# Turning the first two key groups of four attention heads through wider copies, behind the products of the head before

## The chip, the cores and the metric

The kernel runs on one core of a Trainium2 chip. Five engines work on it, each in its own order: PE (TensorE, matrix products and transposes), DVE (VectorE), ACT (ScalarE), POOL (GpSimd) and SP (SyncE, which here issues nearly all DMAs). PE writes to eight PSUM banks; all other tiles lie in SBUF. The metric is the device time of one execution in microseconds (us), and the median of several is compared.

## What is computed

One block of a decoder on x of 1024 tokens by 1024 channels, in float32: attention with a forget gate beside a gated spatial mix, a projection back, and a gated feed-forward network with a short convolution. The part that matters here is the attention, with 8 heads of 64 channels:

```python
def block(args):
    qi, ci, pi = args
    logits = jnp.einsum('bqhd,bkhd->bhqk', qi, k).astype(jnp.float32) * scale
    logits = logits + ci[..., None] - c_k
    causal = pi[:, None] >= key_pos[None, :]
    logits = jnp.where(causal, logits, -jnp.inf)
    p = jax.nn.softmax(logits, axis=-1).astype(v.dtype)
    return jnp.einsum('bhqk,bkhd->bqhd', p, v)
```

The spatial mix and its share of the projection supply independent products that the kernel puts between the attention's own ("filler").

## The kernel before

**Precision.** Products are made of fp32r operands. A float32 value is split into a high part, rounded to fp32r, and the rest (low part); a product is then two or three matmuls.

**One head.** The queries and the keys are cut into 8 blocks of 128. For each query block `j` the logits of its `j + 1` key blocks are two matmuls into PSUM (`logits_mm`, L1021 and L1022), DVE adds the mask and finds the extreme of a row (`logits_min`, L1038), and ACT takes the exponential in place (`logits_exp`, L1062). The rows of the blocks 2i and 2i + 1 lie in one SBUF tile: tags `gg`, `wy`, `t2` and `t3` for i = 0 to 3, in `places`. To multiply them with V, PE has to transpose each 128 x 128 block (`turn_p`): four blocks into one PSUM bank, which ACT casts to the high part (L1094) and DVE subtracts from for the low part (L1095), both into a tile `pt`. Then `values` makes the products with V (L1109), the high part and the low part of a span after each other, into the banks `po`.

**Copies.** A transpose is cheap as fp32r, but an operand of that kind may not be what an engine wrote as float32. So for heads 1 to 7 `copy_p` has SP copy the exponentials by DMA, SBUF to SBUF, into tiles `C2` and `C3` (for i = 2, 3) and new `wy` and `gg` (for i = 1, 0): two DMAs a tile, the odd block of queries first, tile 3 ahead of tile 2. Of `t2` and `t3` only the columns from 256 on are copied (`COLS`). A turn of the first 256 columns, key blocks 0 and 1, for the query blocks 4 to 7 then reads the float32 original with a float32 identity (L1093); all others read the copy as fp32r (L1090).

**The order.** `GROUPS` lists nine groups of turns: key blocks 0 to 7 for the upper half of the queries (the first two are the groups in question), then the lower half. `STEPS` takes two at a time, five steps a head, 40 in all. Step n of the loop at L1226 (head `h`, place `s`) issues the turns of step n + 1, then the products of step n, each followed by logits of head h + 1 (`NEXT`), then exponentials, copies (`due_copies`: tiles 3 and 2 at s = 2, tile 1 at s = 3, tile 0 at s = 4) and, in the places of `FILLS`, one filler of 12 matmuls (L1143 to L1145) with its evacuation (L1147, L1148). At s = 4 stand the turns of head h + 1's first two groups (8 transposes), the four products of the last group (two of 384 columns, two of 128) and a filler. PE keeps the written order (`seq`). On the other engines and on SP a scheduler orders the instructions by its own estimate of when they can run, with some pairs fixed by `after`.

**Also on SP**: `head_loads` (L895 to L908), the filler's residual loads `raw<-xtok` (L1125) and, for each head, the broadcast of the reciprocal row sums from DRAM into `H` (L975), behind ACT's write of them to `rsd` (L974).

**Buffers.** `C2` and `C3` have one buffer each, `pt` three, and the turns, `po` and the row tail share four PSUM banks.

Of the kernel before, what the change touches and what calls it, by code (L numbers as in the profile page):

```python
# [14 lines left out]
P = 128  # L15
# [59 lines left out]
def block_kernel(ctx: ExitStack, tc: tile.TileContext, xT, xtok, wuv, wuh, wv0, wva, wvk, wvl, wqk, cpk, bfv,  # L75
# [225 lines left out]
    for o in (slice(0, 256), slice(256, 512)):  # L301
        h, l, src = xs("B11", 0, 0)[:, o], xs("B11", 1, 0)[:, o], xr("x11", 0)[:, o]
# [657 lines left out]


    TTAG = ("gg", "wy", "t2", "t3")
    COLS = (0, 0, 2, 2)
    CTAG = ("gg", "wy", "C2", "C3")
    exs, turns, due_copies, copied = [], {}, [], []

    def row_tail(h):

        p, hh, rs = h // 2, h % 2, rows[h]
        ptr = bank()  # L970
        rt = idr[0:8, 640 + P * hh:640 + P * (hh + 1)]
        seq(pe.transpose(ptr[0:8, 0:P], rs, ident))
        act.copy(rt, ptr[0:8, 0:P])
        act.dma_start(out=rsd[h], in_=rt)  # L974
        sp.dma_start(out=attF[p][hh * 64:hh * 64 + 64, 1, :],  # L975
                     in_=rsd[h].rearrange("a b -> (a b)").unsqueeze(0).to_broadcast((64, 1024)))
# [71 lines left out]
    def copy_p(h, i, ld=None):  # L1048

        w1, w2 = (2 * i + 1) * P, (2 * i + 2) * P  # L1050
        c = COLS[i] * P
        w1, w2 = w1 - c, w2 - c
        tp = sb(CTAG[i], [P, w1 + w2])
        turns[h, i] = (tp[:, 0:w1], tp[:, w1:w1 + w2])
        for jj in (1, 0):
            copied[:] = [sp.dma_start(out=turns[h, i][jj], in_=places[h, i][jj][:, c:])]
            if ld:
                after(tc, copied[0], ld)
# [21 lines left out]
    def turn_p(g):  # L1080

        ptr = bank()
        pt = sb("pt", [P, 2, 512], F32R)
        for half, k, j0, c, w in spans(g):
            for j in range(j0, 4 * half + 4):
                o = c + (j - j0) * P
                kc = k - COLS[j // 2]
                if kc >= 0 and (g[0], j // 2) in turns:
                    t = turns[g[0], j // 2][j % 2][:, kc * P:(kc + 1) * P]
                    seq(pe.transpose(ptr[:, o:o + P].bitcast(F32R), t.bitcast(F32R), identr))  # L1090
                else:
                    t = places[g[0], j // 2][j % 2][:, k * P:(k + 1) * P]
                    seq(pe.transpose(ptr[:, o:o + P], t, ident))  # L1093
        casts.append(act.copy(pt[:, 0, :], ptr))  # L1094
        los.append(dve.tensor_tensor(out=pt[:, 1, :], in0=ptr, in1=f32(pt[:, 0, :]), op=ALU.subtract))  # L1095
        return pt
# [93 lines left out]
    STEPS = [[(h, g) for g in GROUPS[n:n + 2]] for h in range(8) for n in range(0, 9, 2)]  # L1190
# [34 lines left out]
    turned = [turn_p(g) for g in STEPS[0]]  # L1225
    for n, step in enumerate(STEPS):  # L1226
        h, s = n // 5, n % 5
        if s == 0 and h < 6:
            head_loads(h + 2)
        if h == 7 and s == 0:  # L1230
            for _ in filler:
                pass
            wo_load((0, 1))
            wo_load((2, 3))
        if h in (2, 4, 6) and s == 4:
            for o in (slice(0, 512), slice(512, 1024)):
                pair_half(h // 2 - 1, o)
        now, turned = turned, []
        last, due = due, []
        if n == 0:  # L1240
            fill((0, 0))
        if n == 35:
            psl.release()
            psl = tc.alloc_tile_pool(name="psc", bufs=4, space=bass.MemoryType.PSUM, reuse_waits="tile")
            banks8[0, 0] = lbank()
            wmm(0, 0, banks8[0, 0], (0,))
        for g in STEPS[n + 1] if n + 1 < len(STEPS) else []:
            if n == 36 and turned:
                for e in held + [mrow]:
                    after(tc, logits_exp(*e), casts[-1])  # L1250
            turned.append(turn_p(g))
            if n == 36 and len(turned) == 2:
                after(tc, casts[-1], exs[-1])
        if n == 34:
            mrow = (7, 0, logits_min(7, 0, mrow))
        if n == 33:

            held, last = last, []
        if n == 34:
            last, held = held[:1], held[1:] + last  # L1260
        if n == 35:
            last, held = held[:1], held[1:]
        if s == 1 and h % 2 == 0:
            attF[h // 2] = sb("H", [P, 2, 1024])
        if s == (1 if h < 7 else 2):
            recips[h] = dve.reciprocal(rows[h], rows[h])
        out_copy = None
        if n in EARLY:
            wmm(0, 0, banks8[0, 0], EARLY[n])
        if n == 37:  # L1270
            row_tail(7)
        if n == 39:
            banks8[4, 0] = lbank()
            wmm(4, 0, banks8[4, 0], (0,))
        for c, (g, pt, js) in enumerate(zip(step, now, NEXT[s])):
            out_copy = values(g, pt) or out_copy
            last_copy = out_copy
            if h < 7:
                for j in js:
                    if n == 33 and j == 0:  # L1280
                        mrow = logits_mm(7, 0, place())
                        continue
                    due.append((h + 1, j, logits_min(h + 1, j, logits_mm(h + 1, j, place()))))
            if s == 1 and h < 7 and c == 0:
                row_tail(h)

        for e in last:
            x = logits_exp(*e)
            after(tc, x, casts[-1] if n == 34 else out_copy or casts[-1])
        if s == 2 and h < 7:  # L1290
            due_copies.extend(((h + 1, 3), (h + 1, 2)) if h < 6 else ((7, 3),))
        if n:
            fill((h, s))
        if s > 2 and h < 6:
            due_copies.append((h + 1, 4 - s))
        while due_copies:
            copy_p(*due_copies.pop(0))
        for _ in range(min(len(SPLIT), 1 if n == 9 else 2)):
            ws_, k, wr = SPLIT.pop(0)
            wt = sb("whl", [P, 2, 512], F32R)  # L1300
            ws_[k] = wt
            after(tc, act.copy(wt[:, 0], wr), out_copy or casts[-1])
            pool.tensor_tensor(out=wt[:, 1], in0=wr, in1=f32(wt[:, 0]), op=ALU.subtract)
        if n == 2:
            vh = sb("A", [P, 2, 4, 256])
            sp.dma_start(out=vh, in_=vu.rearrange("h p m c -> p h m c"))
        if n in UPPER:
            tt = UPPER.index(n)
            v = V[tt // 2][:, tt % 2, 4:8]
            src = vh[:, tt // 4, tt % 4, :].rearrange("p (h d) -> p h d", h=4)  # L1310
            after(tc, act.activation(src, src, AF.Copy, scale=rstd1[:, tt:tt + 1]), exs[-1])
            pool.tensor_copy(v[:, :, 0, :], src)
            pool.tensor_tensor(out=v[:, :, 1, :], in0=src, in1=f32(v[:, :, 0, :]), op=ALU.subtract)
# [631 lines left out]
```

## Time and profile before

| | us |
|---|---|
| three runs, median (lowest to highest) | 1041.49 (1040.13 to 1042.59) |
| the profiled execution | 1041.76 |
| its span, first to last instruction | 1039.7 |
| PE busy | 1031.3 (99%) |
| DVE busy | 889.1 (86%) |
| ACT busy | 564.5 (54%) |
| POOL busy | 242.2 (23%) |

The eight heads lie between about 223 and 358 us of the span. In a timeline a row has its start, its length, the engine, the line of the kernel, the operation, the tile written and the tiles read, the shape and the count. Matmuls overlap, so the step between the starts of two rows tells more than their lengths. "SPq" rows are instructions that SP issues. In the rows on DMA the GB/s line has the stretch in 40 equal slices.

### The profile page before, as it was taken

The numbers are of one execution on the slowest core, as the hardware profiler recorded it, in microseconds if no ns is written. First come the engines' busy times: TensorE is split into PE (matmuls) and PEld (weight loads), VectorE is DVE, ScalarE is ACT, GpSimd is POOL, SyncE is SP. The second block draws the span as 40 slices with busy tenths as digits, with TensorE's granted clock in tenths as the row PEclk, the third lists the DMA queues.
The fourth block names the chain that finished last, engine by engine and source line by source line (L and its number), as shares of the span: only waits on it lengthen the run. The fifth ranks groups of instructions, "written<-read, shape, count | busy, mean of one in ns | idle before, by whom it ended". The sixth has DMA issues, their size and how long they took to land.

```text
span 1039.7 us, 14434 instructions
## 1 busy us (share of the span) xinstructions
PE 1031.3 (99%) x4998; PEld 865.5 (83%) x4998; DVE 889.1 (86%) x1294; ACT 564.5 (54%) x1004; POOL 242.2 (23%) x195
## 2 busy tenths in 40 slices
PE   9999999999999999999999999999999999999997
PEld 6988888988888888888888888888888888888886
DVE  6899887888888888998999998998997857997774
ACT  6777533467876757654444443444544554444654
POOL 0000242412633540343334323332331000000000
PEclk9999999999999999999999999999999999999999
DMA  9622558887878652231454332432322998333432
GB/s 336 222 97 82 162 147 245 235 265 225 267 250 255 231 171 93 82 122 62 142 172 144 131 110 72 132 102 89 114 82 94 330 329 293 108 92 101 150 116 100
DMA packets 73708, 170.25 MB, mean 164 GB/s; under 512 B 8718, under 2 KB 12934, under 8 KB 73636
## 3 DMA queue, kind: packets, MB, share of 16 engines
q1 hardware_dynamic: 73364, 169.30, 49.9%
q8 instruction: 39, 0.64, 0.2%
q14 instruction: 33, 0.27, 0.1%
q10 hardware_dynamic: 272, 0.04, 0.0%
HBM read 112.53 MB, written 45.05 MB: 152 GB/s over the span
## 4 chain that ended last, share of the span: by engine, by line
PE 98%; DVE 1%; DMA 1%; issue 0%; SPq 0%; ACT 0%; DVEq 0%
PE pb L1491 23%; PE pk L1491 17%; PE pb L1755 11%; PE pk L1755 9%; PE ps L286 5%; PE pb L286 5%; PE pk L1185 4%; PE pb L1109 3%; PE qc L525 2%; PE qd L525 2%; PE qa L525 2%; PE ps L876 2%; PE pl L1021 1%; PE pl L1022 1%; PE pf L1143 1%; PE pf L1144 1%
## 5 line engine op out<-in xcount | busy, mean ns | idle before, releaser
L1491 PE MATMUL pb<-xT,whb 128*128 128x512 f32 x804 | 189.4, 389 | 0.0
L1491 PEld LDWEIGHTS pb<-xT,whb 128*128 128x128 f32 x804 | 150.9, 188 | 31.4
L1491 PE MATMUL pk<-xB,x 128*128 128x512 f32 x528 | 127.2, 390 | 0.0
L1755 PE MATMUL pb<-whb,x 128*128 128x512 f32 (+1 forms) x528 | 119.2, 387 | 0.0
L1491 PEld LDWEIGHTS pk<-xB,x 128*128 128x128 f32 x528 | 98.8, 188 | 20.8 <-DVE x L175 0.4
L1755 PEld LDWEIGHTS pb<-whb,x 128*128 128x128 f32 x528 | 98.3, 188 | 20.3 <-DVE x L175 0.2
L169 ACT CAST x<-sg 128x512 fp32r<-128x512 f32 x77 | 47.8, 622 | 96.7 <-PE pk L1755 46.1
L169 ACT CAST whb<-sg 128x512 fp32r<-128x512 f32 x82 | 50.5, 617 | 84.8 <-PE pb L1491 83.8
L1755 PE MATMUL pk<-whb,x 128*128 128x512 f32 (+1 forms) x408 | 91.8, 386 | 0.0
L1755 PEld LDWEIGHTS pk<-whb,x 128*128 128x128 f32 x408 | 75.9, 188 | 15.5
L175 DVE TENSOR_TENSOR x<-sg,x 128x512 fp32r<-128x512 f32 x77 | 52.7, 687 | 38.7 <-ACT x L169 38.6
L1541 DVE SCALAR_TENSOR_TENSOR ca<-h,cp,ca 128x1023 f32<-128x1023 f32 (+1 forms) x44 | 68.2, 1550 | 3.7 <-ACT ca L1540 3.6
L1541 DVE SCALAR_TENSOR_TENSOR cg<-h,cp,cg 128x1023 f32<-128x1023 f32 (+1 forms) x44 | 65.2, 1482 | 5.8 <-ACT cg L1540 5.5
L1491 PE MATMUL pb<-xB,whb 128*128 128x512 f32 x264 | 63.9, 389 | 0.0
L175 DVE TENSOR_TENSOR whb<-sg,whb 128x512 fp32r<-128x512 f32 x82 | 57.4, 701 | 4.4 <-ACT whb L169 4.3
L1491 PE MATMUL pk<-xT,whb 128*128 128x512 f32 x252 | 61.0, 389 | 0.0
L1388 POOL TENSOR_TENSOR sg<-raw 128x512 f32<-128x512 f32 x20 | 29.8, 1489 | 131.5 <-DVE whb L175 72.7
L1094 ACT CAST pt<-pb 128x512 fp32r<-128x512 f32 x72 | 40.4, 583 | 33.0 <-PE pb L1090 20.7
L1491 PEld LDWEIGHTS pb<-xB,whb 128*128 128x128 f32 x264 | 49.5, 188 | 10.7 <-issue 0.4
L1095 DVE TENSOR_TENSOR pt<-pb,pt 128x512 fp32r<-128x512 f32 x72 | 47.5, 687 | 11.1 <-ACT pt L1094 10.3
L1491 PEld LDWEIGHTS pk<-xT,whb 128*128 128x128 f32 x252 | 47.2, 188 | 10.0 <-DVE whb L175 0.3
L1109 PE MATMUL pb<-pt,V 128*128 128x512 f32 (+3 forms) x192 | 49.0, 360 | 0.0
(425 smaller groups left out, 2165.7 us busy)
## 6 DMA issues: line engine op xcount, KB each, us to landing
raw<-wup SPq DMA_DIRECT2D x44, 512.0 KB
sg<-hx SPq DMA_DIRECT2D x77, 256.0 KB
hx<-hs SPq DMA_DIRECT2D x44, 256.0 KB
hx<-ca SPq DMA_DIRECT2D x35, 256.0 KB
xT<-wdn SPq DMA_DIRECT2D x28, 256.0 KB
x<-kd SPq DMA_DIRECT2D x18, 256.0 KB
A<-xtok SPq DMA_DIRECT2D x8, 512.0 KB
raw<-wqk SPq DMA_DIRECT2D x8, 512.0 KB
```

The lines of the kernel that those rows point to most:

```text
L169: cast[:] = [act.copy(h, src)]
L175: return eng.tensor_tensor(out=l, in0=src, in1=f32(h), op=ALU.subtract)
L286: pe.matmul(banks[m], xs(n, xi, k)[:, ms], w[:, wi, :], start=(first and k == 0 and c == 0 and (own or m % 2 == 0)), stop=(k == 3 and c == ...
L525: pe.matmul(ps, w[:, wi, ks], xs(n, xi, k), start=(first and c == 0), stop=(c == 11), skip_group_check=True)
L1094: casts.append(act.copy(pt[:, 0, :], ptr))
L1095: los.append(dve.tensor_tensor(out=pt[:, 1, :], in0=ptr, in1=f32(pt[:, 0, :]), op=ALU.subtract))
L1109: seq(pe.matmul(po[half][:, o:o + w], lhs, pt[:, s, c:c + w], start=(new and s == 0), stop=(s == 1 and (half, k) in ((1, 6), (0, 3))), ski ...
L1185: seq(pe.matmul(ps, attT[k][:, a, ts_], w[:, b, :], start=(k == 0 and n == 0), stop=(k == 3 and n == 2)))
L1388: pool.tensor_tensor(out=s[0], in0=a21, in1=a22, op=ALU.add)
L1491: pe.matmul(ps, w[:, wi, ks], xb[:, xi, k, :], start=(first and n == 0), stop=(n == 11), skip_group_check=True)
L1541: return [dve.scalar_tensor_tensor(out=c[:, n:1024], in0=h[:, 0:1024 - n], scalar=w[2 - n], in1=c[:, n:1024], op0=ALU.mult, op1=ALU.add) f ...
L1755: pe.matmul((banks[bk + m] if ps is None else ps)[:, o], xh[:, xi, ms], wh[:, wi, o], start=((first and p_ == 0 or new) and n == 0), stop= ...
```

## The change

For the heads in `FULL`, 1, 2, 3 and 5, the copies into `C2` and `C3` have all columns (1024, 896, 768 and 640 in place of 768, 640, 512 and 384), so that the turns of key blocks 0 and 1 read the copies as fp32r too. For these heads the two turns of the last step of the head before are written behind that step's four products, and ahead of its filler. Heads 4, 6 and 7 keep the former columns and order, and head 0 has no copies.

```diff
-    COLS = (0, 0, 2, 2)
+    FULL = (1, 2, 3, 5)
+
+    def cols(h, i):
+        return 2 if i > 1 and h not in FULL else 0
...
-        c = COLS[i] * P
+        c = cols(h, i) * P
...
-                kc = k - COLS[j // 2]
+                kc = k - cols(g[0], j // 2)
...
-        for g in STEPS[n + 1] if n + 1 < len(STEPS) else []:
+        nxt_ = STEPS[n + 1] if n + 1 < len(STEPS) else []
+        held_back = s == 4 and h + 1 in FULL
+        for g in [] if held_back else nxt_:
...
+        if held_back:
+            turned.extend(turn_p(g) for g in nxt_)
```

Lines of the changed kernel are four (from L968), six (from L1252) or eight (behind the new block) higher than those of before: L1060 is the copy of L1056, L979 the broadcast of L975.

On PE, at the boundary from head 2 to head 3, the last logits of head 3 (into `pl`), the turns (into `pb` banks, by `ident`), the four products (`pt` with `V`) and the first filler matmul (`pf`) stood so:

```order
L1022 MATMUL pl_2896<-x_211_1806,x_210_1805 128x128
L1093 MATMUL pb_2916<-ident,t_414_2791 128x128 x2
L1093 MATMUL pb_2916<-ident,t_402_2748 128x128 x2
L1093 MATMUL pb_2924<-ident,t_414_2791 128x128 x2
L1093 MATMUL pb_2924<-ident,t_402_2748 128x128 x2
L1109 MATMUL pb_2885<-pt_2874,V_1742 128x384 x2
L1109 MATMUL pb_2885<-pt_2874,V_1743 128x128 x2
L1143 MATMUL pf_2940<-whl_2712,G_2035 128x512
```

and stand so in the changed kernel:

```order
L1026 MATMUL pl_2896<-x_211_1806,x_210_1805 128x128
L1113 MATMUL pb_2885<-pt_2874,V_1742 128x384 x2
L1113 MATMUL pb_2885<-pt_2874,V_1743 128x128 x2
L1094 MATMUL pb_2922<-ident,C_432_2855 128x128 x2
L1094 MATMUL pb_2922<-ident,C_431_2852 128x128 x2
L1094 MATMUL pb_2930<-ident,C_432_2855 128x128 x2
L1094 MATMUL pb_2930<-ident,C_431_2852 128x128 x2
L1147 MATMUL pf_2940<-whl_2712,G_2035 128x512
```

The turns went from ahead of the products to behind them, and read the copies `C_432` (tile 2) and `C_431` (tile 3) in place of the originals `t_414` and `t_402`. The other three boundaries read alike.

On SP, at the same boundary, two residual loads, the copies of head 3 and the broadcast into `H` stood so before:

```order
L1125 DMA raw_2850<-xtok 128x512
L1056 DMA C_431_2852<-t_402_2748 128x768
L975 DMA H_2782<-rsd 64x1024
L1056 DMA C_431_2852<-t_402_2748 128x640
L1056 DMA C_432_2855<-t_414_2791 128x512
L1056 DMA C_432_2855<-t_414_2791 128x384
```

and in the changed kernel:

```order
L1129 DMA raw_2850<-xtok 128x512
L979 DMA H_2782<-rsd 64x1024
L1060 DMA C_431_2852<-t_402_2748 128x1024
L1060 DMA C_431_2852<-t_402_2748 128x896
L1060 DMA C_432_2855<-t_414_2791 128x768
L1060 DMA C_432_2855<-t_414_2791 128x640
```

The scheduler moved the broadcast ahead of the first copy. At the boundaries to heads 1, 2 and 5 the broadcast stays between the copies of tile 3 and those of tile 2.

On DVE, at the boundary from head 1 to head 2, the subtractions of the turns (`pt`), the add of the head's output (`H`), the reciprocal of the row sums (`rs`) and the add of the filler (`raw`) stood so before:

```order
L1095 TENSOR_TENSOR pt_2671<-pb_2670,pt_2671 128x512
L1095 TENSOR_TENSOR pt_2679<-pb_2678,pt_2679 128x512
L1118 TENSOR_TENSOR H_2305<-pb_2646,H_2305 64x512
L1266 RECIPROCAL rs_2235<-rs_2235 128x8
L1147 TENSOR_TENSOR raw_2604<-pf_2694,raw_2604 128x512
```

and in the changed kernel:

```order
L1122 TENSOR_TENSOR H_2305<-pb_2646,H_2305 64x512
L1099 TENSOR_TENSOR pt_2677<-pb_2676,pt_2677 128x512
L1099 TENSOR_TENSOR pt_2685<-pb_2684,pt_2685 128x512
L1272 RECIPROCAL rs_2235<-rs_2235 128x8
L1151 TENSOR_TENSOR raw_2604<-pf_2694,raw_2604 128x512
```

The subtractions went behind the add of the head's output; on ACT the casts went behind its copy and one exponential of the next head in the same way.

## The prediction

> **What bounds the kernel now.** I read the chain of waits first, then busy time by stretch over five heads, then what the matrix engine (PE) waits for.
>
> ```profile
> span 1039.7 us, 14434 instructions
> PE 98%; DVE 1%; DMA 1%; issue 0%; SPq 0%; ACT 0%; DVEq 0%
> 258.30:276.20 17.90, 17.88 (x112) 15.36 (x111) 15.03 (x32) 15.00 (x34) 14.41 (x14) 1.00 0.90 277
> 276.20:293.80 17.60, 17.60 (x111) 15.38 (x110) 14.75 (x31) 13.45 (x31) 5.38 (x8) 1.00 0.78 248
> PE pl L1021 <- DVE mn L1038: 0.3, 1, 0.3
> ```
>
> The columns of the two middle rows are the stretch, its length, and the busy time of PE, PE's weight loads, DVE, ACT and POOL, then granted clock, DMA share and GB/s. One head takes 17.6 to 17.9 us and PE is busy for all of it. In the whole attention phase PE waits once, 0.3 us. So here a microsecond taken off PE's stream is a microsecond off the kernel, and a new PE wait is added in full. Nothing later hands it back: 98% of the chain is PE.
>
> **What the change takes off PE.** The row pairs are the boundary from head 1 to head 2, in PE's timeline (start, length, line, operation).
>
> ```profile
> 252.88 0.68 PE L1109 MATMUL pb<-pt,V 128*128 128x384 f32 x4
> 253.40 0.39 PE L1021 MATMUL pl<-x,x 128*128 128x384 f32 x1
> 258.26 1.06 PE L1093 MATMUL pb<-ident,t 128*128 128x128 f32 x8
> 259.07 0.77 PE L1109 MATMUL pb<-pt,V 128*128 128x384 f32 x4
> 259.68 0.45 PE L1143 MATMUL pf<-whl,G 128*128 128x512 f32 x1
> 259.96 0.40 PE L1144 MATMUL pf<-whl,G 128*128 128x512 f32 x1
> 262.51 0.79 PE L1090 MATMUL pb<-ident,C 128*128 128x128 f32 x8
> 263.13 0.69 PE L1109 MATMUL pb<-pt,V 128*128 128x512 f32 x2
> 263.66 0.39 PE L1021 MATMUL pl<-x,x 128*128 128x512 f32 x1
> 264.57 0.61 PE L1109 MATMUL pb<-pt,V 128*128 128x512 f32 x2
> 265.02 0.39 PE L1021 MATMUL pl<-x,x 128*128 128x512 f32 x1
> ```
>
> What counts is the step from one start to the next, since lengths overlap. Eight float32 turns take 259.07 - 258.26 = 0.81 us, the eight fp32r turns 263.13 - 262.51 = 0.62 us. The four products of the last group take 0.61 us behind float32 turns (to 259.68); four products of the same widths behind logits take 0.52 us (252.88 to 253.40). The first filler product now takes 0.28 us. Behind fp32r turns two products take 0.53 us where they take 0.45 us elsewhere (263.13 and 264.57), so I give the filler's 0.23 us the same extra 0.08, 0.31 us. Before: 0.81 + 0.61 + 0.28 = 1.70 us. After: 0.52 + 0.62 + 0.31 = 1.45 us. **Gain 0.25 us at each of four boundaries, 1.0 us.** It can't be much more: if the new turns cost nothing beyond their 0.62 us it is 0.3 each, 1.2 us.
>
> [...]
>
> **What the move does to the engines behind PE.** The four products now start where the turns did. Their first one needs the ACT cast of the last group, their second the DVE subtraction:
>
> ```profile
> 257.66 0.69 DVE L1095 TENSOR_TENSOR pt<-pb,pt 128x512 fp32r<-128x512 f32 x1 [0.22 <-ACT pt L1094]
> 263.33 1.11 ACT L1094 CAST pt<-pb 128x512 fp32r<-128x512 f32 x2
> 263.96 1.29 DVE L1095 TENSOR_TENSOR pt<-pb,pt 128x512 fp32r<-128x512 f32 x2 [0.36 <-ACT pt L1094]
> 268.76 1.07 DVE L1038 CUSTOM_DVE_ANT_0 t<-pl,t,lim 128x768 f32<-128x768 f32 x1
> 270.02 0.39 PE L1021 MATMUL pl<-x,x 128*128 128x512 f32 x1
> 246.25 0.59 ACT L1094 CAST pt<-pb 128x512 fp32r<-128x512 f32 x1 [0.22 <-PE pb L1109]
> 316.24 0.59 ACT L1094 CAST pt<-pb 128x512 fp32r<-128x512 f32 x1 [0.91 <-PE pb L1090]
> ```
>
> The subtraction ends at 258.35; the second product comes at 258.43, since the first, of 384 columns, steps some 0.17 us (three quarters of the 0.23 us of 512 columns). The cover of 0.8 us of turns is gone, 0.08 us is left: cost 0, and up to 0.1 us each if a hand-over takes longer. The new casts and subtractions stand behind the head's output copy and add. ACT has the same work ahead of the casts at 263.33, so they don't move; DVE gets its subtractions at 261.9 instead of 260.7, does the filler's add behind them and is about 0.14 us late with the pair at 263.96. DVE then runs without a pause to 269.83, where PE's logits at 270.02 need the logits tile that it frees. That slack is 0.19 us, and PE comes 0.25 us earlier: about 0.2 us of the gain is lost at this boundary. At the boundaries to heads 1 and 5 I take none off, since ACT pauses ahead of that place (0.22 and 0.91 us, the last two rows). So 1.0 - 0.2 = **0.8 us of gain**.
>
> **What the wider copies cost.** Each of the four copies has 256 columns more, 0.52 MB a head; their DMA is paid by PE only if the turns wait for it. Before, the first turn that reads the copies is the one at 262.51. Now it is the one that starts where the products end, 0.52 us behind these four rows:
>
> ```profile
> 240.66 1.06 PE L1093 MATMUL pb<-ident,t 128*128 128x128 f32 x8
> 276.17 1.06 PE L1093 MATMUL pb<-ident,t 128*128 128x128 f32 x8
> 311.44 1.06 PE L1093 MATMUL pb<-ident,t 128*128 128x128 f32 x8
> 233.87 1.31 SPq L1056 DMA_DIRECT2D C<-t  x2
> 251.60 1.38 SPq L1056 DMA_DIRECT2D C<-t  x2
> 254.79 1.28 SPq L1056 DMA_DIRECT2D C<-t  x2
> 269.58 0.49 SPq L1056 DMA_DIRECT2D C<-t  x1
> 271.84 0.46 SPq L975 DMA_DIRECT2D H<-rsd  x1
> 272.39 1.87 SPq L1056 DMA_DIRECT2D C<-t  x3
> 304.79 1.38 SPq L1056 DMA_DIRECT2D C<-t  x2
> SPq L975 <- DMA rsd<-t: 1.7, 1, 1.7
> GB/s 25 351 401 401 401 376 401 401 401 385 439 355 376 397 397 334 343 268 334 502 468 134 101 33 0 0 0 351 334 451 318 418 251 105 364 351 364 326 213 201
> DMA packets 665, 1.48 MB, mean 302 GB/s; under 512 B 80, under 2 KB 208, under 8 KB 665
> DMA packets 758, 1.67 MB, mean 264 GB/s; under 512 B 80, under 2 KB 208, under 8 KB 757
> GB/s 328 232 205 218 198 143 178 191 184 266 417 386 417 389 369 154 14 246 382 261 213 227 179 265 364 403 369 394 400 367 273 96 0 218 341 266 14 14 61 358
> ```
>
> The needs are thus 241.18, 258.78, 276.69 and 311.96 (turns of heads 1, 2, 3, 5), and the first turn reads the copy that lands last. The fifth DMA in their midst, the broadcast of row sums into H, goes through the same queue. Together 128 x (1024 + 896 + 768 + 640) x 4 bytes = 1.70 MB and 0.26 MB, **1.97 MB**. The two packet rows are the stretches 252.6 to 257.5 and 234.9 to 241.2, in which mostly the same five DMAs of before went through, at a mean of 302 and 264 GB/s; the first GB/s row is the former stretch in 40 slices, of which many are near 400. At 302 GB/s 1.97 MB take 6.5 us, at 400 GB/s 4.9 us; the wider copies leave fewer gaps than the old ones, so I take 350 GB/s, 5.6 us.
>
> - Head 2: data flow from the second slice, 252.7, 1.1 us behind the issue at 251.60; in by 258.3 (257.6 to 259.2), need 258.78: no wait (0 to 0.4).
> - Head 1: issue at 233.87, so data from 235.0; in by 240.6, need 241.18. At the 264 GB/s that this stretch had, 242.4. I take 0.4 us (0 to 1.2).
> - Head 5: issue at 304.79, data from some 306.0; in by 311.6 (310.9 to 312.5), need 311.96: 0.1 us (0 to 0.5).
> - Head 3: **the order on SP has changed**. Before, the first copy was issued at 269.58 and the H broadcast behind it, at 271.84, after 1.7 us of waiting for the row sums' own write. Now H stands ahead of all four copies, so SP is held until 271.84 and the copies follow from 272.4. The last quoted row (slices of 0.3 us from 268.0) shows the queue run dry at 272.8 and H's data start at 273.1. From there 5.6 us: in by 278.7 (278.0 to 279.6), need 276.69: **2.0 us of PE wait** (1.3 to 2.9).
>
> PE is in order: behind the waiting turn stand its filler products and all of the next head, so the wait is paid whole. What a later copy delays beyond that (loads of the next heads' operands, half a head ahead of use) I cost at nothing, by the 0.3 us of waits that PE has in all.
>
> [...]
>
> **The sum.** -0.8 + 0.4 + 0 + 2.0 + 0.1 = +1.7 us. The profiled execution took 1041.76 us (span 1039.7 and 2.1 around it), so 1043.5; the median shown, 1041.49, is 0.27 below it, and on the median's footing the forecast is **1043.2 us**, 0.16% slower. About 0.2%, 2.1 us, is what a measurement of this kernel can tell from no change.
>
> **Rivals.**
>
> - *All copies are in time.* The transfers run near 400 GB/s, and the new order on SP costs less than it seems. For it: slices of 380 to 417. Against it: head 3 misses by 1.3 us even at 400. It gives -0.6 to -1.0: 1040.5 to 1040.9.
> - *Late in several places*, the slower side. The mechanism is the landing of the last wide copy at the means seen: at 302 GB/s (264 for head 1) the waits are 1.2 + 0.4 + 2.9 + 0.5 = 5.0, less 0.8: +4.2, 1045.7. It shows as slower (over +2.1) as soon as the mean rate falls under some 340 GB/s, where head 3 waits 2.2 and head 1 0.7 us. For it: three stretches of quoted rates below that. Against it: those hold gaps between smaller copies. [...]
> - *The turns don't get cheaper*: the fp32r step of 78 ns comes from the later groups, whose loads and neighbours differ. Then the gain is 0.1 a boundary and the sum +2.1. The order of instructions shows that the turns do read the copies.
> - *Faster by more than 0.2%* would need 2.1 us where the whole gain is 1.0 to 1.2; no row gives it.
>
> **How the numbers follow.** The forecast (one clear wait at head 3, +0.8 to +3.0) 0.57, copies in time 0.18, late in several places 0.18, no cheaper turns 0.04, faster 0.03. Of the forecast's case some 0.2 of the 0.57 lie above +2.1, so slower 0.2 + 0.18 + 0.02 = 0.40, faster 0.03, and 0.57 within 0.2%. The range runs from all copies in time, 1040.5, to the middle of the late case, 1045.0.
>
> **What would show it.** In the changed profile PE should have a wait in front of the first turn of head 3, ended by the DMA into C, of 1.3 to 2.9 us, and at most small ones at heads 1, 2 and 5. The eight turns should step 0.62 us, the four products ahead of them 0.52 us. On SP the H broadcast near 271.5 should be followed by four copies, and H should be what SP waits for. A head 3 without that wait, or PE waits for DVE of 0.5 us or more, would make the forecast wrong.

## The result, and the profile after

The changed kernel takes **1053.61 us** (median of 4 runs, 1052.14 to 1054.45) against 1041.7 us before (the median of four runs, the three above and one more): ratio 1.0111, 95% interval 1.0099 to 1.0123, so 11.9 us slower. The forecast was 1043.2 us, range 1040.5 to 1045.0: **wrong**, with the right sign of its one clear wait and far too small a size. The profiled execution took 1052.14 us.

First the page of the changed kernel (span, the chain of waits by engine) and the one new row in what PE waited for (total us, times, longest us):

```profile
span 1050.1 us, 14425 instructions
PE 94%; DMA 3%; ACT 1%; DVE 1%; issue 1%; SPq 0%; ACTq 0%; DVEq 0%
```

```profile
PE pb L1094 <- DMA C<-t: 8.5, 4, 4.2
```

PE was 98% of the chain and is 94%; DMA rose from 1% to 3%. The first turn waits for the wide copies, four times, 8.5 us in all, once at each boundary. PE's timeline shows them in the order of the heads, the last products (x4) and the turns (x8), with the wait in brackets, and behind head 3 a few filler products:

```profile
240.92 0.83 PE L1113 MATMUL pb<-pt,V 128*128 128x384 f32 x4
243.22 0.87 PE L1094 MATMUL pb<-ident,C 128*128 128x128 f32 x8 [1.48 <-DMA C<-t]
260.15 0.77 PE L1113 MATMUL pb<-pt,V 128*128 128x384 f32 x4
262.34 0.88 PE L1094 MATMUL pb<-ident,C 128*128 128x128 f32 x8 [1.42 <-DMA C<-t]
279.27 0.77 PE L1113 MATMUL pb<-pt,V 128*128 128x384 f32 x4
284.24 1.17 PE L1094 MATMUL pb<-ident,C 128*128 128x128 f32 x8 [4.20 <-DMA C<-t]
285.76 0.63 PE L1148 MATMUL pf<-whl,G 128*128 128x512 f32 x1
286.19 0.63 PE L1149 MATMUL pf<-whl,G 128*128 128x512 f32 x1
287.88 0.39 PE L1147 MATMUL pf<-whl,G 128*128 128x512 f32 x1
288.10 0.39 PE L1148 MATMUL pf<-whl,G 128*128 128x512 f32 x1
320.25 0.76 PE L1113 MATMUL pb<-pt,V 128*128 128x384 f32 x4
322.39 0.87 PE L1094 MATMUL pb<-ident,C 128*128 128x128 f32 x8 [1.38 <-DMA C<-t]
331.16 0.27 PE L976 MATMUL pb<-ident,rs 128*8 128x128 f32 x1
```

The last row, the transpose of head 5's row sums, stood at 320.88 before (L972). It is 10.28 us later; the span grew by 10.4, so nearly all of the loss lies ahead of it. Each boundary's share comes from the starts of the slot behind the last logits (before: the float32 turns at 240.66, 258.26, 276.17, 311.44; now the x4 rows):

| boundary to head | 1 | 2 | 3 | 5 |
|---|---|---|---|---|
| slot later than before, us | 0.26 | 1.89 | 3.10 | 8.81 |
| added at this boundary (next minus this) | 1.63 | 1.21 | 5.71 | 1.47 |
| PE's wait | 1.48 | 1.42 | 4.20 | 1.38 |
| wait in the forecast | 0.4 | 0 | 2.0 | 0.1 |

The waits explain the shares but for head 3, where 1.5 us more are lost. There the filler's products step 0.43 us (285.76 to 286.19) where they step 0.22 behind 287.88. The busy time by stretch shows why (stretch, its length, busy us of PE, PE's loads, DVE, ACT and POOL, granted clock, DMA share, GB/s):

```profile
281.02:284.43 3.41, 0.19 (x2) 0.19 (x3) 0.89 (x2) 2.11 (x7) 2.60 (x6) 1.00 1.03 395
284.43:287.85 3.42, 3.42 (x14) 2.89 (x14) 1.29 (x2) 1.09 (x2) 0.71 (x1) 0.50 1.07 342
```

For 3.41 us behind the long wait PE was granted half its clock (the 0.50), so half of that time, 1.7 us of work, is lost.

### The profile page after: what moved, and what is told of

The parts are those of the page before. It is cut to its first block, busy times and chain, and to the rows that moved or that the text cites. A ratio compares the mean times of both kernels' runs of the same rounds, so it can differ in the third digit from the quotient of the medians.

```text
span 1050.1 us, 14425 instructions
## 1 busy us (share of the span) xinstructions
PE 1032.9 (98%) x4998; PEld 866.7 (83%) x4998; DVE 889.8 (85%) x1294; ACT 564.5 (54%) x1004; POOL 241.9 (23%) x195
## 4 chain that ended last, share of the span: by engine, by line
PE 94%; DMA 3%; ACT 1%; DVE 1%; issue 1%; SPq 0%; ACTq 0%; DVEq 0%
PE pb L1499 23%; PE pk L1499 17%; PE pb L1763 11%; PE pk L1763 9%; PE ps L286 5%; PE pb L286 5%; PE pk L1189 4%; PE qc L525 2%; PE qd L525 2%; PE pb L1113 2%; DMA C<-t 2%; PE qa L525 2%; PE ps L876 2%; PE pb L1094 1%; PE pf L1147 1%; PE pf L1149 1%
```

## The experiments

Ratios are to the kernel before, with 95% intervals.

### What costs: the bytes, the move, or the wait?

**Wide copies, nothing moved.**

```diff
-                if kc >= 0 and (g[0], j // 2) in turns:
+                if (k > 1 or j < 4) and (g[0], j // 2) in turns:
...
-        held_back = s == 4 and h + 1 in FULL
+        held_back = False
```

> The copies of heads 1, 2, 3 and 5 stay wide and the scheduler keeps the broadcast ahead of them at head 3, but the turns of the first two groups read the float32 originals again, ahead of the four products. Theory A (what costs is PE's wait for the landing of the wide copies, at the moved place): nothing reads the copies before the third group, some 3.5 us later, so the three waits of about 1.4 us are gone and at head 3 at most 1 us of the 4.2 us is left, with no stretch at half clock: 1041 to 1043 us. Rival B (the 0.52 MB more a head crowd the DMA queue and delay other loads, wherever the turns stand): 1046 us or more, with PE waits in other places.

Measured: 1042.7 us, ratio 1.0008 (0.9998 to 1.0018), as theory A has it. The one wait for a copy that is left is that of head 3's third group:

```profile
281.57 0.85 PE L1094 MATMUL pb<-ident,C 128*128 128x128 f32 x8 [0.95 <-DMA C<-t]
```

**The move alone.**

```diff
-        return 2 if i > 1 and h not in FULL else 0
+        return 2 if i > 1 else 0
```

> Only the move: the first two groups of heads 1, 2, 3 and 5 are turned behind the four products, but from the float32 originals, and all copies keep their former columns. Theory A: the originals are there long before, so no wait for a DMA; the products step some 0.52 in place of 0.61 us, 0.1 us less at a boundary, and DVE gives at most 0.2 us back: 1041 to 1042 us, the same as before. Rival C (the move itself costs, since the four products lose the cover of the turns and wait for DVE's subtraction, and the next head's products get their casts later): 0.5 us or more a boundary, 1043.5 us or more, with PE waiting for DVE.

Measured: 1041.51 us, ratio 0.9995 (0.9984 to 1.0005). PE's timeline at the boundary to head 2:

```profile
257.68 0.76 PE L1113 MATMUL pb<-pt,V 128*128 128x384 f32 x4
258.27 1.06 PE L1097 MATMUL pb<-ident,t 128*128 128x128 f32 x8
259.08 0.47 PE L1147 MATMUL pf<-whl,G 128*128 128x512 f32 x1
259.40 0.39 PE L1148 MATMUL pf<-whl,G 128*128 128x512 f32 x1
```

No wait, but no gain either: products 0.59, turns 0.81, first filler 0.32, together 1.72 us against 1.70 before. Neither the bytes nor the move costs more than about 1 us (the 0.95 us wait); rivals B and C fall. What costs is that the turns, at their new place, wait for the copies.

### Head 3: the place of the broadcast

**Heads 1, 2 and 5 alone.**

```diff
-    FULL = (1, 2, 3, 5)
+    FULL = (1, 2, 5)
```

> The change for heads 1, 2 and 5 alone; head 3 as before the change. Theory A, by boundary (net delays read off the two traces: head 1 1.6, head 2 1.2, head 3 5.7, head 5 1.5 us): 5.7 us less than the changed kernel, about 1047.9 us, the three waits of about 1.4 us unchanged and no half clock. Rival D (the loss is spread alike over the four heads, and the half clock would come anyway, from some other place): three quarters of the loss, about 1050.5 us.

Measured: 1046.55 us, ratio 1.0043 (1.0032 to 1.0054), 7.1 us less than the changed kernel: head 3 has more than half of the loss, and rival D falls on that. Theory A's time, 1047.9 us, is missed too: it had the three waits unchanged, and they are 1.50, 1.32 and 0.78 us. And the half clock did come from another place, which theory A denied. In its profiled execution it follows the 1.50 us wait of head 1, first in PE's timeline, then by stretch:

```profile
242.58 1.05 PE L1094 MATMUL pb<-ident,C 128*128 128x128 f32 x8 [1.50 <-DMA C<-t]
```

```profile
239.61:243.02 3.41, 1.91 (x15) 1.59 (x14) 2.77 (x7) 2.94 (x9) 0.00 (x0) 1.00 0.87 297
243.02:246.44 3.42, 3.42 (x13) 2.84 (x12) 1.40 (x3) 2.29 (x6) 1.84 (x4) 0.50 0.57 207
```

**The broadcast behind the copies at head 3.** `BEHIND` names the heads whose copies go first.

```diff
+    BEHIND = (3,)
...
-        sp.dma_start(out=attF[p][hh * 64:hh * 64 + 64, 1, :], ...)
+        def spread():
+            return sp.dma_start(out=attF[p][hh * 64:hh * 64 + 64, 1, :], ...)
+
+        if h + 1 in BEHIND:
+            spreads.append(spread)
+        else:
+            spread()
...
         while due_copies:
             copy_p(*due_copies.pop(0))
+        if s == 2 and spreads:
+            after(tc, spreads.pop()(), copied[0])
```

> The change with all four heads, but at head 3 the broadcast of the row sums is issued behind the four copies. Theory A (SP, held by the broadcast, starts the copies 6 us late there, and the 4.2 us wait then halves PE's clock): the first copy is issued near 269.5 us of the span, PE's wait at head 3 falls to between 0.5 and 2 us, the clock stays whole, and 3.5 to 5 us of the 5.7 go: 1048.5 to 1050 us. Rival E (the copies of head 3 are late for another reason: the exponentials that they read, or the transfer rate): the wait stays near 4 us and the time near 1053 us.

Measured: 1047.36 us, ratio 1.0053 (1.0033 to 1.0073), 6.2 us less than the changed kernel and 1 us below the range of theory A. SP's and PE's timelines of it, behind those of the changed kernel on SP:

```profile
269.38 2.06 SPq L1129 DMA_DIRECT2D raw<-xtok  x2
275.67 0.45 SPq L979 DMA_DIRECT2D H<-rsd  x1
276.22 3.41 SPq L1060 DMA_DIRECT2D C<-t  x4
```

```profile
273.25 4.57 SPq L1067 DMA_DIRECT2D C<-t  x4
```

```profile
281.18 0.87 PE L1101 MATMUL pb<-ident,C 128*128 128x128 f32 x8 [0.52 <-DMA C<-t]
```

In the changed kernel SP issues nothing from 271.4 to 275.67, held by the broadcast (4.1 us of this is its wait for the row sums' own write), and the four copies follow. With the broadcast behind them (at 279.49 us) they start 3 us sooner, the wait falls from 4.20 to 0.52 us and no half clock follows there; one follows head 1's wait of 1.36 us. Rival E falls. (The first copy came at 273.25, not at 269.5: it then waits for its exponentials.)

### Heads 1, 2 and 5: one DMA engine of sixteen

The DMA view of the changed kernel, 241.2 to 243.2 us in slices of 0.05 us (busy share of the 16 engines in tenths, then GB/s), and the row on instruction fetches of 235 to 243.4 us (packets, MB, share):

```profile
DMA  8969979775121111119999991040109919919579
GB/s 328 563 246 430 369 287 553 287 307 205 41 103 41 51 41 41 51 41 215 82 461 246 297 82 51 0 133 0 51 0 614 246 41 614 328 41 532 246 287 410
q8 instruction: 1, 0.02, 0.7%
```

From 241.7 to 242.1 us one engine of sixteen works (one or two tenths, some 41 GB/s); the other fifteen have nothing to do, and PE waits until 243.22. In the midst of these copies, at 237.8 us, a 16 KB instruction fetch took 0.94 us of one engine. The trace lists the packets of the transfers; the last copy of a head is 128 packets of 2560 bytes, one a row, so eight for each of the sixteen engines by an estimate (an even share):

| boundary to head | 1 | 2 | 3 | 5 |
|---|---|---|---|---|
| PE could start the turn (its start less the wait) | 241.74 | 260.92 | 280.04 | 321.01 |
| 120 of the 128 packets had landed | 241.50 | 260.46 | 283.40 | 321.00 |
| the last eight had landed | 242.72 | 261.82 | 283.72 | 321.86 |
| the turn starts | 243.22 | 262.34 | 284.24 | 322.39 |

At heads 1, 2 and 5 the last eight go one after another, some 0.1 us each, which fits one engine; it ends 1.22, 1.36 and 0.86 us behind the rest; at head 3 no engine stands out. And at all four the turn starts 0.50 to 0.53 us behind the last packet. The trace doesn't name a packet's engine; whether the late one is that of the fetch, the next run tests.

**The fetch moved** ahead of the copies of heads 1 and 2, by cutting the products of the first four fillers in two:

```diff
+                    for e, (a, b) in enumerate(((0, 0), (0, 1), (1, 0))):
+                        m = 2 if hf == 0 and tt < 4 else 1
+                        for c in range(m):
+                            cs = slice(c * 512 // m, (c + 1) * 512 // m)
-                    seq(pe.matmul(ps, sgT[k][:, 0, ts_], w[:, 0, :], start=(k == 0), stop=False))
...
+                            seq(pe.matmul(ps[:, cs], sgT[k][:, a, ts_], w[:, b, cs], ...))
```

> The changed kernel, with the 48 products of the first four fillers, ahead of head 1, cut into two of 256 columns: the same computation, 48 matmuls and as many weight loads more on PE (some 2 to 4 us more, not part of the question). In the trace of the changed kernel an instruction fetch of 16 KB stands in the queue of one DMA engine at 237.8 and again at 258.5 us, in the midst of the copies of heads 1 and 2, and that engine ends its part of the last copy some 1.2 us behind the other fifteen. These fetches come every 21 us, so about 250 PE instructions apart; 96 more move them about 8 us ahead of the copies. Theory F (the fetch makes one of sixteen engines late, and PE waits for that one): the waits at heads 1 and 2 fall from 1.48 and 1.42 us to 0.2 to 0.6 us. Rival G (the mean rate and the time from the last byte to the semaphore make the waits): they stay at 1.3 to 1.5 us. Head 5 stays near 1.4 us by G; by F it stays too, unless the other fetch there moves as well.

Measured: one run, 1050.87 us. The fetches went through at 230.4 and 251.0 us instead of 237.8 and 258.5. In PE's timeline head 1 waits 0.44 us, head 2 shows no wait, and head 5 waits 1.61 us:

```profile
242.56 0.88 PE L1094 MATMUL pb<-ident,C 128*128 128x128 f32 x8 [0.44 <-DMA C<-t]
260.24 0.87 PE L1094 MATMUL pb<-ident,C 128*128 128x128 f32 x8
320.75 0.88 PE L1094 MATMUL pb<-ident,C 128*128 128x128 f32 x8 [1.61 <-DMA C<-t]
```

Theory F holds and G falls: some 1.0 us of head 1's wait and nearly all of head 2's came from the fetch. The part of G that stays is the time from the last packet to the turn, 0.49 us at head 1 here too. At head 5 the cut had the opposite effect: a 16 KB fetch that went through at 308.0 us in the changed kernel now falls among the copies, at 317.8, and the wait grew from 1.38 to 1.61 us. What makes an engine late at head 5 in the changed kernel itself is not shown: only an 8 KB fetch of another queue lies in its copies, at 316.3 us, and it took 0.31 us.

### Giving the copies more time

**The turns in the middle of the filler,** behind its sixth product:

```diff
         if held_back:
-            turned.extend(turn_p(g) for g in nxt_)
+            MID.append(lambda: turned.extend(turn_p(g) for g in nxt_))
...
                 for k in range(4):
+                    if k == 2 and MID:
+                        MID.pop()()
                     w = whs[k]
```

> The change, but the two turns stand behind the sixth of the twelve filler products that follow, 1.4 us of PE work later. Theory A: the copies get 1.4 us more, so the waits at heads 1, 2 and 5 fall to at most 0.2 us, and at head 3 from 4.2 to 2.8 us, below the length that halves the clock: 1.4 us at each of three boundaries, and 1.4 + 1.7 at head 3, 7.3 us less than the changed kernel: 1046 us (1045 to 1047). Rival H (the casts and subtractions now come too late for the next step's products, 2 us behind the turns): PE waits for ACT or DVE instead, 0.5 us or more a boundary, 1048 us or more. Rival I (the half clock at head 3 doesn't come from the length of the wait): it stays, and the time is 1.7 us above theory A.

Measured: 1046.6 us, ratio 1.0038 (1.0025 to 1.0052), within theory A's range. The waits at heads 1, 2 and 5 are gone from PE's list and head 3 waits 2.56 us, with a whole clock in the profiled execution (PE's timeline, then by stretch):

```profile
280.52 0.85 PE L1094 MATMUL pb<-ident,C 128*128 128x128 f32 x8 [2.56 <-DMA C<-t]
```

```profile
278.86:282.27 3.41, 1.75 (x13) 1.60 (x14) 0.70 (x2) 1.82 (x4) 2.19 (x4) 1.00 0.96 331
282.27:285.69 3.42, 3.42 (x22) 2.89 (x21) 3.10 (x6) 1.17 (x2) 0.00 (x0) 1.00 0.79 228
```

But that execution, 1043.87 us, is the fastest of five. Three others, of 1046.6 to 1047.4 us, have mean clocks of 0.997 or 0.998 where it has 0.999. Their profiles weren't taken, but clock and time point to a half clock in at least two of them. So the median meets theory A's sum in part by luck, and rival I doesn't fall. Nor does any run show a length of wait that halves the clock, which theory A's sum takes for granted: waits of 1.36 and 1.50 us were followed by half clock, this one of 2.56 us was not.

**That, and the broadcast behind the copies at all four heads** (`BEHIND = (1, 2, 3, 5)`):

> Both: the turns in the middle of the filler, and the broadcast of the row sums behind the copies of heads 1, 2, 3 and 5. Theory A: no wait for a DMA of over 0.2 us is left at the four boundaries, the cheaper turns show at last, and the time is that of the kernel before less 0.2 to 0.8 us: 1040.6 to 1041.4 us. Rival H (late casts): 1043 us or more, with PE waiting for ACT or DVE at the boundaries.

Measured: 1046.37 us, ratio 1.0044 (1.0031 to 1.0057). **The broadcast behind the copies at all four heads, the turns where the change put them:**

> The change, with the broadcast behind the copies at all four heads, and the turns where the change put them. Theory A (the last copy lands as late as the bytes ahead of it in the queue make it): 0.26 MB less ahead of it at some 350 GB/s is 0.75 us, so the waits at heads 1, 2 and 5 fall from 1.4 to about 0.7 us, head 3 waits 0.5 us as with the broadcast moved there alone, and the time is that kernel's 1047.4 less 2.1 us: 1045.2 us. Rival J (the copies of tile 2 can't be issued earlier, since they wait for their exponentials, so nothing comes sooner at heads 1, 2 and 5): waits of 1.2 to 1.4 us, 1047 us.

Measured: 1048.38 us, ratio 1.0061 (1.0046 to 1.0077). Both miss. In the first no wait for a copy is left; in the second those of heads 1, 2 and 5 are 0.85, 0.49 and 0.35 us, so the copies do land sooner, against rival J. But both have a new wait, of 2.36 us, that no theory had. From the second, PE's timeline, then POOL's:

```profile
278.08 0.50 PE L1155 MATMUL pf<-whl,G 128*128 128x512 f32 x1 [2.36 <-POOL whl L1320]
```

```profile
265.92 2.54 POOL L995 TENSOR_TENSOR H<-H 128x512 f32<-128x512 f32 x2
276.76 1.26 POOL L1320 TENSOR_TENSOR whl<-raw,whl 128x512 fp32r<-128x512 f32 x1
```

POOL multiplies by the broadcast row sums (L995). It did so from 261.05 in the changed kernel and does from 265.92 here, behind the later broadcast, and the split of the next filler's weights behind it ends at 278.0 instead of 275.8. The broadcast that was only in the way at head 3 was needed at head 2. PE also waits for DVE's subtractions, as rival H has it: 0.74 and 0.65 us behind the turns of heads 2 and 3 in the first, 0.67 us behind those of head 3 in the second (and in both runs of the next paragraph).

**The turns in the filler, the broadcast behind at head 3 alone** (`BEHIND = (3,)`):

> The turns in the middle of the filler, and the broadcast behind the copies at head 3 alone (behind them at heads 1 and 2 it made a weight load late and PE wait 2.4 us for POOL). Theory A: no wait for a copy of over 0.2 us is left at any boundary, no stretch at half clock, and none of the waits for POOL; from the span with the turns in the filler alone, 1041.9, its one wait of 2.56 goes: span 1039.3, time 1041.4 us (1040.8 to 1042.2), at most 0.5 us below the kernel before, since the late casts give part of the 0.25 us a boundary back. Rival K (the wide copies crowd the queue even when nothing waits for them): 1043 us or more.

Measured: 1044.49 us, ratio 1.0028 (1.0019 to 1.0038). A miss; the time is rival K's, the cause another: the scheduler now put the broadcast at head 5 between the two copies of tile 3, and head 5 waits 1.22 us. **Six heads** (`FULL = (1, 2, 3, 4, 5, 6)`, `BEHIND = (3, 4, 5, 6)`):

> As the run before, for heads 1 to 6, with the broadcast behind the copies at heads 3 to 6. Theory A: two more boundaries of 0.25 us less what late casts cost: 1041.0 us (1040.4 to 1042), not to be told from the run before. Rival L (a broadcast that moves, or the two heads' wider copies, delays another load, as the wait for POOL showed): 1043 us or more, with a PE wait of over 1 us for POOL or DVE behind such a load.

Measured: 1047.07 us, ratio 1.0044 (1.0031 to 1.0057). No wait for a copy is left, but one of 2.0 us for ACT and one of 1.2 us for DVE behind the heads: rival L. **The turns in the filler for heads 1, 2 and 5 alone:**

> The turns in the middle of the filler, for heads 1, 2 and 5 alone; nothing of the broadcasts is moved, and head 3 is as before the change. Theory A: no wait for a copy of over 0.2 us, no half clock, and three boundaries with the cheaper turns, less what late casts cost (0.24 us once with the turns in the filler): 1041.2 us (1040.5 to 1042), within 0.1% of the kernel before. Rival K (the wide copies or the late casts cost something at every head): 1042.5 us or more.

Measured: 1042.65 us, ratio 1.0005 (0.9996 to 1.0014): 0.65 us above theory A's range, and in rival K's. PE's list has no wait for a DMA on the heads and none for POOL, and the clock is whole; still there is no gain. PE's timeline has the last product ahead of head 2's turns with these turns, then the boundary to head 5:

```profile
260.13 0.39 PE L1151 MATMUL pf<-whl,G 128*128 128x512 f32 x1
260.66 0.85 PE L1094 MATMUL pb<-ident,C 128*128 128x128 f32 x8
311.80 0.77 PE L1113 MATMUL pb<-pt,V 128*128 128x384 f32 x4
312.41 0.45 PE L1149 MATMUL pf<-whl,G 128*128 128x512 f32 x1
312.69 0.40 PE L1150 MATMUL pf<-whl,G 128*128 128x512 f32 x1
313.85 0.79 PE L1094 MATMUL pb<-ident,C 128*128 128x128 f32 x8
314.47 0.47 PE L1149 MATMUL pf<-whl,G 128*128 128x512 f32 x1
314.78 0.40 PE L1150 MATMUL pf<-whl,G 128*128 128x512 f32 x1
```

At head 2 the product ahead of the turns steps 0.53 us where such a product steps 0.23, and at head 1 it steps 0.52. So PE still waits 0.3 us at each for the last copy, whose last packets landed at 242.20 and 260.05 us, 0.6 us ahead of the turns; the list is blind to this, since idle time counts only from the modelled end of the product. Behind head 2's turns the next eight step 0.95 us in place of 0.62, which fits late casts. From boundary to boundary heads 1 and 2 take 0.34 and 0.30 us longer than before, which is rival K's cost at two of the three heads.

At head 5 nothing waits: products 0.61, first filler product 0.28, turns 0.62, and 0.08 that the product behind them takes over its 0.23: 1.59 us against 1.70. At the place where the change put the turns the one boundary without a wait, head 3 in the run with all four broadcasts behind, has 0.60 + 0.68 + 0.31 = 1.59 us too. The cheaper turns are worth some 0.1 us a boundary.

### The half clock

**Work in the wait of head 3:**

```diff
+        if g == STEPS[15][0]:
+            for _ in range(8):
+                seq(pe.matmul(ptr, abs_[3][0][:, 0:P], abs_[3][1][:, 0:512], start=True, stop=True))
```

> The changed kernel, with eight products of 512 columns added ahead of the first turn of head 3, in the bank that the turn then overwrites: work that nothing uses, 1.84 us in the midst of the 4.2 us wait. Theory W (the clock is judged by how much PE streams in fixed windows of 3.41 us): the wait falls to 2.3 us, no window is left nearly empty at head 3, no stretch of half clock follows there, and the kernel with more work is 1.7 us faster than the changed kernel: about 1051.5 us. Rival M (the half clock belongs to the place or to the wait for a DMA, not to PE's lack of work): it stays, and the time is 1053.5 us.

Measured: 1053.7 us, ratio 1.0100 (1.0079 to 1.0122). Theory W's time is missed: the copies were issued 1.2 us later and landed later, the added products ended by 283.3, and the window behind them was nearly empty. A second half clock followed head 2's wait of 1.83 us. The stretches:

```profile
259.44:262.85 3.41, 1.58 (x16) 1.43 (x14) 2.40 (x7) 3.16 (x10) 2.40 (x4) 1.00 0.96 253
262.85:266.27 3.42, 3.42 (x10) 2.68 (x9) 1.40 (x3) 1.95 (x5) 3.35 (x4) 0.50 0.89 331
283.33:286.74 3.41, 0.67 (x8) 0.68 (x8) 0.35 (x2) 1.17 (x5) 2.42 (x5) 1.00 0.90 323
286.74:290.16 3.42, 3.42 (x11) 2.74 (x10) 1.29 (x2) 1.02 (x2) 0.00 (x0) 0.50 0.71 237
```

This fits both theories. Its four runs say more: three had a mean clock of 0.995 or 0.996 and took 1053.6 to 1054.4 us, one had 1.000 and took 1049.56. So the place alone doesn't bring the half clock.

**Work in all four waits:** five products ahead of the turns of heads 1, 2 and 5, twelve at head 3.

```diff
+        if g in [STEPS[5 * h][0] for h in FULL]:
+            for _ in range(12 if g[0] == 3 else 5):
+                seq(pe.matmul(ptr, abs_[g[0]][0][:, 0:P], abs_[g[0]][1][:, 0:512], start=True, stop=True))
```

> The changed kernel with products added that nothing uses, in the bank that the first turn then overwrites: five of 512 columns (1.15 us) ahead of the turns of heads 1, 2 and 5, twelve (2.8 us) ahead of those of head 3. The added instructions let the scheduler issue one copy of head 3 ahead of the broadcast, and move the instruction fetches. Theory W (a window of 3.41 us in which PE streams less than about 1.2 us is followed by one at half clock): no window falls under that, the granted clock is 1.000 or 0.999 in every run, and the time is that of the changed kernel without its half clock: 1049 to 1050.5 us, 3 to 4 us less although PE does 27 products more. Rival M (the half clock belongs to the place or to the wait for a DMA): clocks of 0.994 to 0.998 and 1052 us or more.

Measured: 1049.72 us, ratio 1.0083 (1.0067 to 1.0098), clocks 0.999 to 1.000 in all four runs. Head 3 in PE's timeline:

```profile
279.21 2.98 PE L1090 MATMUL pb<-x,x 128*128 128x512 f32 x12
282.03 0.80 PE L1097 MATMUL pb<-ident,C 128*128 128x128 f32 x8
```

With 27 products more the kernel is 3.9 us faster than the changed kernel, and no half clock is left, as theory W has it. Its bound of about 1.2 us no run shows: by PE's busy time in stretches of 3.41 us, the one with 1.91 us was followed by half clock (heads 1, 2 and 5 alone), the one with 1.75 us was not (the turns in the filler). The run can't tell PE's lack of work from the wait for a DMA, since no such wait of over 0.3 us is left in it; what speaks against the wait as such is the one of 2.56 us above, behind which the clock stayed whole. Not all of the 3.9 us is the clock: here one copy of head 3 was issued ahead of the broadcast, and nothing waits behind the twelve products.

## Why the prediction was wrong

- **What bounds the kernel: right.** PE is the path; a new PE wait was paid in full, 8.5 us of them.
- **The gain, 0.25 us a boundary: too large.** The runs show 0.11 us (1.59 against 1.70). The 0.52 us for the four products was read off a row behind wide logits; here they stand behind logits of 128 columns and take 0.59 to 0.61 us, as before the change. The turns' 0.62 us is right between wide products; behind the products of 128 columns they take 0.68, and behind a wait 0.71 to 0.72. The rival without cheaper turns had the size, 0.1 us, by luck: the turns are cheaper. In the changed kernel even this doesn't show, as each wait is 0.17 us longer than its row says (it counts from the modelled end of the products, 0.77 us behind their start; they step 0.60). So 0.8 us of the sum wasn't there.
- **What the wider copies cost, heads 1, 2 and 5: the step that failed first.** "Start + 1.97 MB / 350 GB/s" gives the time at which the queue as a whole is done, and this it gave not badly: fifteen engines were done 0.24, 0.46 and 0.01 us ahead of PE's need, and the forecast had 0.58, 0.48 and 0.35. But PE waits for the last of sixteen engines, 1.22, 1.36 and 0.86 us later, and for 0.50, 0.52 and 0.53 us from the last packet to the turn. The forecast put both terms at nothing. With them the waits come out as 1.48, 1.42 and 1.38 us. With the fetch out of the way the waits at heads 1 and 2 are 0.44 and about 0 us, the forecast's 0.4 and 0; at head 1 that is luck, since its 0.4 was set between the 0 of its own rate and the 1.2 of 264 GB/s. (Nor do the 0.7 us that a rival gives head 1 at 340 GB/s follow from the formula, which has no wait there.) A late engine could be seen before the change. These are the GB/s of the kernel before, of 234.9 to 241.2 us, of which the prediction used only the mean, 264:

```profile
GB/s 117 351 390 371 468 371 390 397 341 423 358 276 302 355 250 198 390 338 104 273 312 286 195 221 286 384 341 371 173 46 13 13 13 26 26 23 254 393 345 390
```

From 239.5 to 240.6 us 13 to 46 GB/s are left, about the work of one engine (some 41 GB/s in the changed kernel, above), behind a 16 KB fetch at 237.6 us. What pulls the mean down is not a slow queue but a late engine.

- **Head 3: right mechanism, half the size.** The broadcast held SP, as foreseen, but SP was released 3.6 us ahead of the products (275.67 against 279.27) where the forecast took 4.3 (271.84 against 276.17), and the copies took 8.0 us from issue to the turn (276.22 to 284.24) where it took 6.3. Data flowed 1.0 us behind the issue instead of 0.7, and for 6.5 us (277.2 to 283.72) instead of 5.6; the last 0.5 us are again those from the last packet to the turn. The rate wasn't the trouble: 2.19 MB went in these 6.5 us, near 340 GB/s, but 0.22 MB of them were other copies, and the forecast counted 1.97 MB. The rows, of 276.2 to 284.3 us, so with what came behind the last copy too:

```profile
GB/s 0 0 0 0 0 182 263 324 263 263 283 344 142 222 142 202 263 344 364 445 346 465 389 336 478 352 432 412 334 445 364 400 394 359 384 400 415 405 405 402
DMA packets 891, 2.42 MB, mean 299 GB/s; under 512 B 95, under 2 KB 96, under 8 KB 890
```

- **The clock: not in the sum.** The half clock cost 1.7 us in the profiled execution, behind a wait of 4.20 us; other runs had it behind 1.36 and 1.50 us. The three other runs of the changed kernel have mean clocks of 0.994 to 0.996 instead of 0.998, one or two such stretches more by an estimate (each takes 0.0016 off the mean).
- **The sum.** Forecast +1.7 us, measured +10.4 in the profiled execution: waits 8.5 in place of 2.5 (6.0), the clock 1.7, the missing gain 0.8; together 8.5 of the 8.7 us between them. The rival "late in several places" had the places and 5.0 us of waits, but by a slower mean rate, not by a late engine; its chance of 0.18 was too small, and even it left out the half clock, which followed waits of 1.36 to 4.20 us in these runs.

No version tried beats the kernel before: the best two (the move alone, the turns in the filler for three heads) can't be told from it. What the change could win, four times 0.1 us, is less than these runs can tell from nothing (the interval of the move alone is 0.1% to either side).

## What to carry to other kernels

When PE is the path and a step is moved to a transfer's landing, count to the last DMA engine, add what one instruction fetch costs it (here 1.2 to 1.4 us) and the half microsecond from the last packet to the reader, instead of bytes over the mean rate; by an estimate from these numbers (1.22 + 0.50) a margin of under 1.7 us is a wait where a fetch falls among the copies. A list of waits can be blind to 0.3 us of them: compare steps too. Read the order that the scheduler makes on the issuing engine: one DMA that waits for another transfer holds all those behind it (4.1 us here), and moving it can starve its own reader (2.36 us). Take a step's price from a place with the same neighbours, since the same eight turns took 0.62, 0.68 or 0.72 us.

## What the runs showed of the hardware

- A fetch of 16 KB of instructions is one packet and took 0.94 and 1.04 us here (at 237.8 and 258.5 us); of the 128 packets of the last copy around it, the last eight landed 1.22 and 1.36 us behind the rest, and with the fetch moved the copy ended 0.3 and 0.2 us behind the rest.
- Between the last packet of a copy and the start of the turn that waits for it lie 0.50 to 0.53 us at the four boundaries of the changed kernel, and 0.48 to 0.61 us in all waits for a wide copy in these runs but one (1.51 us, at head 5 with the broadcast behind at all four heads).
- Eight turns of 128 x 128 step 0.81 us as float32, and 0.62 to 0.72 us as fp32r, by what stands ahead of them.
- The stretches of half clock quoted here last 3.41 us. Two starts in one execution lay a whole number of these apart: 262.85 and 286.74 (the work in the wait of head 3) 7.00 times 3.413 us, and in the changed kernel 284.43 and 1049.02, near the span's end, 224.0 times.
- A wait need not be long for it. Waits of 1.36 us (the broadcast moved at head 3; its head 1) and 1.50 us were followed by half clock, one of 2.56 us was not. How little PE must do stays open: 1.91 us of busy time in 3.41 us was followed by half clock and 1.75 us was not (the quoted rows of heads 1, 2 and 5 alone, and of the turns in the filler).
- The runs of one kernel differ by it: with heads 1, 2 and 5 alone, five runs with a mean clock of 0.997 took 1046.5 to 1047.3 us, four with 0.999 took 1044.1 to 1045.9 (the tenth, with 0.998, 1047.0).
